# A hybrid decoder layer on one core: weights and mixed heads turned by VectorE and transfers instead of TensorE

## The chip, the cores and the metric

One core of a Trainium2 chip. The metric is the device time of one execution in microseconds (us). TensorE (PE) multiplies, with its weight loads (PEld) beside it; VectorE (DVE), ScalarE (ACT) and GpSimd (POOL) work on tiles; SyncE (SP) and POOL issue DMAs. Each engine takes its own list of instructions in order and waits on semaphores of the others.

## The reference

Cut to what is computed (x is 256 x 2048, one layer, 8 heads in each group):

```
h    = rmsnorm(x, ln1);  dq, dk, dv, sq, sk, sv = split(h @ w_in)          # 2048 x 6144
diff = softmax(q1 k1) v - lam * softmax(q2 k2) v      # causal, partial rotary on q and k
diff = rmsnorm(diff, per head) * (1 - lam_init)
a    = exp(log_sigmoid(z) + sum of log_sigmoid(-z) over later keys)        # strictly causal
sb   = rmsnorm(a @ sv, per head)
x    = x + concat(diff, sb) @ w_out                                        # 2048 x 2048
h    = rmsnorm(x, ln2);  x = x + relu(h @ w_mlp_in)**2 @ w_mlp_out         # 2048 x 8192 x 2048
out  = rmsnorm(x, ln_f)
```

## The kernel before

Every large product is fp32 split in two: an operand is hi + lo, and hi*hi, hi*lo and lo*hi are summed in PSUM (lines L260, L261, L262). The weights stream in as chunks of 512 rows by 512 columns (1 MB, tile w) into three buffers. Half a chunk is one job: ScalarE casts it into wh (L214), VectorE subtracts for wl (L217), and TensorE does 12 products of 128x512. Casts run three jobs ahead of the products, into four buffers each of wh and wl. Jobs 0 to 95 are the input projection, twelve blocks of eight jobs in the order dq0 dk0 dv0 dq1 dk1 dv1 sq0 sk0 sv0 sq1 sk1 sv1 (the digit is a group of four heads). From job 96 on comes the output projection: columns 0 and 1 (of four) with the rows of mixed heads 0 to 5 (jobs 96 to 107), then their last rows, which need mixT6 and mixT7 (jobs 108 to 111), then columns 2 and 3. The MLP follows.

Attention runs beside these jobs, as generators in a queue called side. After each job `tick` lets the first two of them run to their next yield; in jobs 96 to 107 it did so twice. What is called then only fixes the order in which instructions are handed over: a planner places them by a simulated time line, so an instruction that waits for its inputs there gets a later place in its engine's list.

- `prep_task` turns a q or k block: VectorE transposes blocks of 32x32 into the tile bl (L373, one buffer), 16 DMAs put them in place (L378, half from SP, half from POOL), and ScalarE copies the result into T (L396).
- `diff_task` does one head after another: scores (L443, L449), softmax of both maps and their difference w (L453 to L470), three TensorE transposes of w into PSUM (wtp, L475), a ScalarE copy to wT (L477), and the products with the values (L490).
- `sb_task` does two heads at once: scores (L503, L506), log of the break probabilities (L512 to L519), prefix sums by TensorE (L523 to L527), exponential (L531), values (L490).
- `finish_pair` normalises the output of two heads (L418 to L424), transposes it on TensorE (mtp, four transposes, L428), and splits it with the head gain into mixT (`split_pair`, L156 and L157).

Names carry a digit for group and head: s10 is the first head pair of the second stick-breaking group, s11 the second pair. mixT0 to mixT3 come from the softmax heads, mixT4 to mixT7 from the others; s10 makes mixT6 and s11 mixT7.

Of the kernel before, what the change touches and what calls it, by code (L numbers as in the profile page):

```python
# [10 lines left out]
F32 = mybir.dt.float32  # L11
# [7 lines left out]
P = 128  # L19
S = 256  # L20
D = 2048
DFF = 4 * D
NT = S // P
KT = D // P
NB = 512
CK = 4
HK = 2
HG = 4
# [16 lines left out]
def tile_hybrid_layer(  # L45
# [21 lines left out]
    nc = tc.nc  # L67
# [28 lines left out]
    ident = cpool.tile([P, P], F32, name="ident")  # L96
# [104 lines left out]
    def issue_conv():  # L201
        i = state["conv"]
        if i >= len(jobs):
            return
        c, h, _, _, pools = jobs[i]
        state["conv"] += 1
        if c is None:
            return
        w = wt[c][:, h * HK:(h + 1) * HK, :]
        pool = mlp["split"] if "split" in mlp and i % 3 == 2 else spool  # L210
        ph, pl = pools or ((pool, "wh"), (pool, "wl"))
        wh = ph[0].tile([P, HK, NB], F32R, tag=ph[1], name=f"wh{i}")
        for j in (range(HK) if i == 0 else (slice(0, HK),)):
            state["wh"] = nc.scalar.copy(wh[:, j], w[:, j])  # L214
        wl = pl[0].tile([P, HK, NB], F32R, tag=pl[1], name=f"wl{i}")
        for j in (range(HK) if i == 0 else (slice(0, HK),)):
            state["wl"] = nc.vector.tensor_tensor(wl[:, j], w[:, j], wh[:, j].bitcast(F32), op=ALU.subtract)  # L217
        sp[i] = (wh, wl)
        if h == CK // HK - 1:
            del wt[c]  # L220
            issue_dma()
# [4 lines left out]
    def tick(n=2):  # L226
        for task in list(side)[:n]:
            try:
                next(task)
            except StopIteration:  # L230
                side.remove(task)

    def run_jobs(upto, nside=2):
        while state["job"] < upto:
            i = state["job"]
            if i in hooks:
                hooks[i]()
            while state["conv"] < min(i + 1 + state["ahead"], len(jobs)):
                issue_conv()
            c, h, products, after, _ = jobs[i]  # L240
            products(h, *sp.pop(i, (None, None)))
            if after is not None:
                after()
            tick(nside)
            if n_proj <= i < n_out0:
                tick(nside)
            state["job"] += 1

# [26 lines left out]
    ps_tp = ctx.enter_context(tc.tile_pool(name="ps_tp", bufs=1, space=PSUM))  # L275
    attn = ExitStack()
    ap_ = attn.enter_context(tc.tile_pool(name="attn", bufs=2))
    ps_sc = attn.enter_context(tc.tile_pool(name="ps_sc", bufs=1, space=PSUM))
    ps_o = attn.enter_context(tc.tile_pool(name="ps_o", bufs=1, space=PSUM))
# [18 lines left out]
    ghd = cpool.tile([P, 1], F32, name="ghd")  # L298
    lamc = cpool.tile([P, 2], F32, name="lamc")
    epsc = cpool.tile([P, 1], F32, name="epsc")  # L300
    mostc = cpool.tile([P, 1], F32, name="mostc")
# [67 lines left out]
    def turn(dst, bl, src, engines):  # L369
# [6 lines left out]
        for i in range(4):  # L376
            for f in range(4):
                engines[(i * 4 + f) % len(engines)].dma_start(  # L378
                    dv[f * 32:(f + 1) * 32, :, i, :], bl[i * 32:(i + 1) * 32, :, f, :])


    grp = {}

# [30 lines left out]
    def finish_pair(o, g, kt2, name, **norm):  # L414

        ov = o.rearrange("p (g c) -> p g c", c=P)
        sq = ap_.tile([P, 4, P], F32, tag="sq", name=f"sq_{name}", bufs=1)
        nc.scalar.activation(sq, ov, AF.Square)  # L418
        ss = tiny.tile([P, 4], F32, tag="hss", name=f"hss_{name}")
        nc.vector.tensor_reduce(ss, sq, axis=AX.X, op=ALU.add)  # L420
        r = tiny.tile([P, 4], F32, tag="hr", name=f"hr_{name}")
        rsqrt_mean(ss, 4, P, name, r, **norm)
        on = ap_.tile([P, 4, P], F32, tag="on", name=f"on_{name}", bufs=1)
        nc.vector.tensor_tensor(on, ov, r.unsqueeze(2).broadcast_to([P, 4, P]), op=ALU.mult)  # L424
        yield
        tp = ps_tp.tile([P, 2 * S], F32, tag="tp", name=f"mtp_{name}")
        for i in range(4):
            nc.tensor.transpose(tp[:, i * P:(i + 1) * P], on[:, i, :], ident)  # L428
        yield
        mixT[kt2] = apool.tile([P, HK, 2, S], F32R, tag="act", name=f"mixT{kt2}")  # L430
        split_pair(mixT[kt2], tp, g, False)

    def diff_task(gi):
        while f"dk{gi}" not in grp:
            yield

        qT, kT, v = grp[f"dq{gi}"], grp[f"dk{gi}"], grp[f"dv{gi}", "src"]
        for h in range(HG):
            nm = f"d{gi}{h}"
            sc = ps_sc.tile([P, 2, 512], F32, tag="sc", name=f"sc_{nm}")  # L440

            for m in range(2):
                nc.tensor.matmul(sc[:, m, P:3 * P], identb, dmask, start=True, stop=False,  # L443
                                 skip_group_check=True)
            for cs, qs, ks, last in ((slice(0, S), slice(P, S), slice(0, S), False),
                                     (slice(S, S + P), slice(0, P), slice(0, P), True)):
                for m in range(2):
                    dm = slice(m * 64, (m + 1) * 64)
                    nc.tensor.matmul(sc[:, m, cs], qT[dm, h, qs], kT[dm, h, ks],  # L449
                                     start=False, stop=last, skip_group_check=True)  # L450
            yield
            nm4 = tiny.tile([P, 2, 2], F32, tag="nmax", name=f"nmax_{nm}")
            nc.vector.tensor_reduce(nm4[:, 1, :], sc[:, :, 0:S], axis=AX.X, op=ALU.max, negate=True)  # L453
            nc.vector.tensor_reduce(nm4[:, 0, :], sc[:, :, S:S + P], axis=AX.X, op=ALU.max, negate=True)
            e = ap_.tile([P, 2, 3 * P], F32, tag="e", name=f"e_{nm}", bufs=2)
            es = tiny.tile([P, 2, 2], F32, tag="es", name=f"es_{nm}")
            segs = {1: slice(0, S), 0: slice(S, S + P)}
            for qt in (1, 0):
                for m in range(2):
                    nc.scalar.activation(e[:, m, segs[qt]], sc[:, m, segs[qt]], AF.Exp,  # L460
                                         bias=nm4[:, qt, m:m + 1],
                                         accum_out=es[:, qt, m:m + 1])
            er = tiny.tile([P, 2, 2], F32, tag="er", name=f"er_{nm}")
            nc.vector.reciprocal(er, es)
            nc.vector.tensor_tensor(er, er, lamc.unsqueeze(1).broadcast_to([P, 2, 2]), op=ALU.mult)
            w = e[:, 0, :]
            for qt in (1, 0):
                s = segs[qt]
                nc.vector.tensor_scalar_mul(e[:, 1, s], e[:, 1, s], er[:, qt, 1:2])
                nc.vector.scalar_tensor_tensor(w[:, s], w[:, s], er[:, qt, 0:1], e[:, 1, s],  # L470
                                               op0=ALU.mult, op1=ALU.add)
            yield
            tp = ps_tp.tile([P, 2 * S], F32, tag="tp", name=f"wtp_{nm}")
            for i in range(3):
                nc.tensor.transpose(tp[:, i * P:(i + 1) * P], w[:, i * P:(i + 1) * P], ident)  # L475
            wT = ap_.tile([P, 3 * P], F32, tag="wT", name=f"wT_{nm}")
            nc.scalar.copy(wT, tp[:, :3 * P])  # L477
            yield
            if h % 2 == 0:
                o = ps_o.tile([P, 512], F32, tag="o", name=f"o_{nm}")  # L480
            pv_products(o, h, [wT[:, S:S + P]], [wT[:, 0:P], wT[:, P:S]], v)
            if h % 2 == 1:
                yield
                yield from finish_pair(o, ghd, (gi * HG + h) // 2, nm, eps=epsc, most=mostc)

    def pv_products(o, h, lhs0, lhs1, v):
        for qt, lhs in ((0, lhs0), (1, lhs1)):
            c0 = ((h % 2) * 2 + qt) * P
            for kb, l in enumerate(lhs):
                nc.tensor.matmul(o[:, c0:c0 + P], l, v[:, kb, h * P:(h + 1) * P],  # L490
                                 start=kb == 0, stop=kb == len(lhs) - 1)
# [86 lines left out]
    n_proj = len(jobs)  # L578
# [51 lines left out]
    n_out0 = len(jobs)  # L630
# [202 lines left out]
    with tc.manual_schedule(engines={mybir.EngineType.PE, mybir.EngineType.Activation, mybir.EngineType.DVE}):  # L833
        state["ahead"] = 0
        keep_clock_up(WARM0, "a")
        for step in START_ORDER.split():
            {"x": x_pair, "c": lambda i: issue_conv(), "m": lambda i: run_jobs(i + 1)}[step[0]](int(step[1]))
    state["ahead"] = AHEAD
    run_jobs(n_out0)
    while any(m is None for m in mixT):  # L840
        tick()
# [61 lines left out]
```

## Time and profile before

| | |
|---|---|
| median of three runs | 1110.95 us (1110.37 to 1111.13) |
| the profiled execution | 1109.93 us |
| its span, first to last instruction | 1108.2 us |
| TensorE busy | 1095.4 us, 99% |
| VectorE, ScalarE, POOL busy | 647.8, 519.4, 121.0 us |
| chain that ended last | PE 98% of the span |

The page gives for each engine the time in which it worked on something. A line of a timeline gives start and duration in us, engine, source line, operation, written tile <- read tiles, shape, count, and in brackets how long the engine had stood before it and who released it. Products are pipelined: one of 128x512 is shown with 0.39 us, while the next one starts 0.23 us after it; the distance of two starts is what one costs.

### The profile page before, as it was taken

How to read it: one execution, taken by the hardware profiler on the slowest of the kernel's cores; microseconds unless marked ns; L12 is line 12 of the kernel's file. 1: busy time of each engine (PE TensorE's matmuls, PEld its weight loads, DVE VectorE, ACT ScalarE, POOL GpSimd, SP SyncE). 2: the span in 40 equal slices, each digit the busy share in tenths (PEclk: the TensorE clock that was granted, in tenths of full speed). 3: DMA queues.
4: the chain of work that ended last, by engine and by line, in shares of the span. 5: the costliest groups of instructions: out<-in, count | busy, mean ns of one | idle time of the engine just before them, and what ended most of it. 6: DMA issues, size and time to landing. Idle time of an engine off the chain costs nothing.

```text
span 1108.2 us, 13750 instructions
## 1 busy us (share of the span) xinstructions
PE 1095.4 (99%) x5019; PEld 905.7 (82%) x5019; DVE 647.8 (58%) x798; ACT 519.4 (47%) x665; POOL 121.0 (11%) x240
## 2 busy tenths in 40 slices
PE   8999999999999999999999999999999999999996
PEld 6887888888887888888888888888888888888886
DVE  5756766656456665565554665545566544655752
ACT  5655555555555554444333444333444333444541
POOL 1111101101100212230001111000211000131000
PEclk9999999999999999999999999999999999999999
DMA  8675555646646885765666765656676566667512
GB/s 293 203 252 168 184 181 162 197 155 188 208 153 230 312 257 176 260 224 197 198 193 195 240 215 191 210 190 194 188 248 215 196 197 198 214 192 247 191 38 77
DMA packets 130296, 222.35 MB, mean 201 GB/s; under 512 B 11282, under 2 KB 26676, under 8 KB 130100
## 3 DMA queue, kind: packets, MB, share of 16 engines
q1 hardware_dynamic: 122772, 213.59, 58.3%
q0 software_dynamic: 7168, 7.35, 2.6%
q8 instruction: 39, 0.64, 0.2%
q10 hardware_dynamic: 288, 0.52, 0.1%
q14 instruction: 29, 0.24, 0.1%
HBM read 204.65 MB, written 2.10 MB: 187 GB/s over the span
## 4 chain that ended last, share of the span: by engine, by line
PE 98%; DMA 0%; DVE 0%; ACT 0%; SPq 0%; issue 0%; DVEq 0%; ACTq 0%
PE ia L260 10%; PE ia L262 10%; PE ia L261 10%; PE ma L261 10%; PE ma L262 10%; PE ma L260 10%; PE oacc L260 3%; PE oacc L262 3%; PE oacc L261 3%; PE acc_dk L260 1%; PE acc_dq L261 1%; PE acc_sk L260 1%; PE acc_sq L260 1%; PE acc_dq L262 1%; PE acc_sk L261 1%; PE acc_dq L260 1%
## 5 line engine op out<-in xcount | busy, mean ns | idle before, releaser
L217 DVE TENSOR_TENSOR wl<-w,wh 128x1024 fp32r<-128x1024 f32 (+1 forms) x385 | 468.7, 1221 | 393.7 <-ACT wh L214 392.7
L214 ACT CAST wh<-w 128x1024 fp32r<-128x1024 f32 (+1 forms) x385 | 402.2, 1049 | 501.8 <-PE ia L262 196.8
L261 PE MATMUL ia<-wl,xs 128*128 128x512 f32 x512 | 199.0, 389 | 0.0
L262 PE MATMUL ia<-wh,xs 128*128 128x512 f32 x512 | 198.6, 389 | 0.0
L260 PE MATMUL ia<-wh,xs 128*128 128x512 f32 x512 | 198.5, 389 | 0.0
L260 PE MATMUL ma<-wh,aT 128*128 128x512 f32 x480 | 186.3, 389 | 0.0
L261 PE MATMUL ma<-wl,aT 128*128 128x512 f32 x480 | 186.3, 389 | 0.0
L262 PE MATMUL ma<-wh,aT 128*128 128x512 f32 x480 | 185.5, 389 | 0.0
L378 POOL DMA_DIRECT2D hT<-bl x128 | 67.4, 535 | 529.9 <-DMA w<-in_w_mlp_in_dram 244.3
L262 PEld LDWEIGHTS ia<-wh,xs 128*128 128x128 f32 x512 | 96.1, 188 | 20.0
L261 PEld LDWEIGHTS ia<-wl,xs 128*128 128x128 f32 x512 | 96.1, 188 | 19.9
L260 PEld LDWEIGHTS ia<-wh,xs 128*128 128x128 f32 x512 | 96.1, 188 | 19.9
L260 PEld LDWEIGHTS ma<-wh,aT 128*128 128x128 f32 x480 | 90.1, 188 | 18.7
L261 PEld LDWEIGHTS ma<-wl,aT 128*128 128x128 f32 x480 | 90.1, 188 | 18.7
L262 PEld LDWEIGHTS ma<-wh,aT 128*128 128x128 f32 x480 | 90.1, 188 | 18.7
L260 PE MATMUL oacc<-wh,mixT 128*128 128x512 f32 x128 | 49.9, 391 | 1.3 <-ACT mixT L156 1.3
L261 PE MATMUL oacc<-wl,mixT 128*128 128x512 f32 x128 | 50.1, 392 | 0.0
L262 PE MATMUL oacc<-wh,mixT 128*128 128x512 f32 x128 | 49.4, 389 | 0.0
L378 POOL DMA_DIRECT2D x2T<-x2bl x32 | 16.8, 534 | 114.6 <-DVE x L615 72.7
L260 PEld LDWEIGHTS oacc<-wh,mixT 128*128 128x128 f32 x128 | 24.0, 188 | 6.3 <-ACT mixT L156 1.5
L261 PEld LDWEIGHTS oacc<-wl,mixT 128*128 128x128 f32 x128 | 24.1, 188 | 4.9
L262 PEld LDWEIGHTS oacc<-wh,mixT 128*128 128x128 f32 x128 | 24.0, 188 | 4.8
(227 smaller groups left out, 1219.9 us busy)
## 6 DMA issues: line engine op xcount, KB each, us to landing
w<-in_w_mlp_in_dram SPq DMA_DIRECT2D x64, 1024.0 KB, 5.4
w<-in_w_mlp_out_dram SPq DMA_DIRECT2D x64, 1024.0 KB, 5.1
w<-in_w_in_dram SPq DMA_DIRECT2D x46, 1024.0 KB, 5.1
w<-in_w_out_dram SPq DMA_DIRECT2D x16, 1024.0 KB, 5.4
hT<-bl SPq DMA_DIRECT2D x128, 32.0 KB, 1.9
hT<-bl POOLq DMA_DIRECT2D x128, 32.0 KB, 1.8
w<-in_w_in_dram SPq DMA_DIRECT2D x4, 512.0 KB, 7.7
x<-in_x_dram SPq DMA_DIRECT2D x3, 512.0 KB, 10.1
```

Of the source, the lines that this page charges most:

```text
L214: state["wh"] = nc.scalar.copy(wh[:, j], w[:, j])
L217: state["wl"] = nc.vector.tensor_tensor(wl[:, j], w[:, j], wh[:, j].bitcast(F32), op=ALU.subtract)
L260: nc.tensor.matmul(acc[t], a[:, 0, st], wh[:, j, :], start=s0, stop=False)
L261: nc.tensor.matmul(acc[t], a[:, 0, st], wl[:, j, :], start=False, stop=False)
L262: state["mm"] = nc.tensor.matmul(acc[t], a[:, 1, st], wh[:, j, :], start=False, stop=s1)
L378: engines[(i * 4 + f) % len(engines)].dma_start(dv[f * 32:(f + 1) * 32, :, i, :], bl[i * 32:(i + 1) * 32, :, f, :])
```

## The change

The three weight transposes on TensorE and the copy behind them are replaced by `turn_blocks`: one VectorE transpose of 32x32 blocks into the used second half of the tile e, and 16 DMAs (eight on SP, eight on POOL) straight into wT. The mixed heads are turned in the same way, through the tile bl and back into on, for all pairs but the last (mixT7), which keeps its TensorE transposes. Values products run one head behind the weights, since a turn now takes a round trip. In jobs 96 to 107 the queue is called four times a job instead of twice.

```diff
-            if n_proj <= i < n_out0:
+            for _ in range(3 if n_proj <= i < n_out0 else 0):
                 tick(nside)
...
+    def turn_blocks(dst, bl, src, n):
+        nc.vector.transpose(bl.rearrange("p f (k b) -> p f k b", b=32),
+                            src.rearrange("p (k f a) -> p f k a", k=n, f=4))
+        dv = dst.rearrange("p (k i b) -> p k i b", k=n, i=4)
+        for i in range(4):
+            for f in range(4):
+                (nc.gpsimd if f % 2 else nc.sync).dma_start(
+                    dv[f * 32:(f + 1) * 32, :, i, :],
+                    bl[i * 32:(i + 1) * 32, f, :].rearrange("a (k b) -> a k b", b=32))
...
-        yield
-        tp = ps_tp.tile([P, 2 * S], F32, tag="tp", name=f"mtp_{name}")
-        for i in range(4):
-            nc.tensor.transpose(tp[:, i * P:(i + 1) * P], on[:, i, :], ident)
+        if kt2 == KT // HK - 1:
+            yield
+            tp = ps_tp.tile([P, 2 * S], F32, tag="tp", name=f"mtp_{name}")
+            for i in range(4):
+                nc.tensor.transpose(tp[:, i * P:(i + 1) * P], on[:, i, :], ident)
+        else:
+            bl = ap_.tile([P, NT, 4, 4 * 32], F32, tag="bl", name=f"mbl_{name}", bufs=1)
+            tp = on.rearrange("p g c -> p (g c)")
+            turn_blocks(tp, bl[:, 0], tp, 4)
+            yield
+            yield
         yield
...
+        def values(h, nm, wT):
+            if h % 2 == 0:
+                o[0] = ps_o.tile([P, 512], F32, tag="o", name=f"o_{nm}")
+            pv_products(o[0], h, [wT[:, S:S + P]], [wT[:, 0:P], wT[:, P:S]], v)
+            if h % 2 == 1:
+                yield
+                yield from finish_pair(o[0], ghd, (gi * HG + h) // 2, nm, eps=epsc, most=mostc)
...
-            tp = ps_tp.tile([P, 2 * S], F32, tag="tp", name=f"wtp_{nm}")
-            for i in range(3):
-                nc.tensor.transpose(tp[:, i * P:(i + 1) * P], w[:, i * P:(i + 1) * P], ident)
+            bl = e[:, 1, :].rearrange("p (f c) -> p f c", f=4)
             wT = ap_.tile([P, 3 * P], F32, tag="wT", name=f"wT_{nm}")
-            nc.scalar.copy(wT, tp[:, :3 * P])
-            yield
-            if h % 2 == 0:
-                o = ps_o.tile([P, 512], F32, tag="o", name=f"o_{nm}")
-            pv_products(o, h, [wT[:, S:S + P]], [wT[:, 0:P], wT[:, P:S]], v)
-            if h % 2 == 1:
-                yield
-                yield from finish_pair(o, ghd, (gi * HG + h) // 2, nm, eps=epsc, most=mostc)
+            turn_blocks(wT, bl, w, 3)
+            yield
+            if last is not None:
+                yield from values(*last)
+            last = (h, nm, wT)
+        yield
+        yield
+        yield
+        yield from values(*last)
```

Where instructions stand now is shown at three places. The first is ScalarE's list around the copy T_sk1, the turned keys of the second stick-breaking group (the number behind wh is that of the half chunk, and so of the job that it serves). Before:

```order
L214 CAST wh94_2631<-w47_2525 128x1024
L214 CAST wh95_2647<-w47_2525 128x1024
L396 COPY T_sk1_2665<-src_sk1_2555 128x1024
L214 CAST wh96_2676<-w48_2562 128x1024
L214 CAST wh97_2701<-w48_2562 128x1024
L512 ACTIVATE t_s10_2692<-sc_s10_2667 128x768
```

The same list of the changed kernel around the same copy:

```order
L156 ACTIVATE mixT5_2729<-on_s01_2654,g2T_426 128x2x256
L214 CAST wh105_3131<-w52_2922 128x1024
L214 CAST wh106_3151<-w53_3025 128x1024
L214 CAST wh107_3167<-w53_3025 128x1024
L214 CAST wh108_3185<-w54_3101 128x1024
L407 COPY T_sk1_2839<-src_sk1_2726 128x1024
L214 CAST wh109_3201<-w55_3135 128x1024
```

The copy has moved from behind cast 95 to behind cast 108. The second place is TensorE's list at the prefix sums of s10 (negone and negtri_r are constants; oacc is the output projection). Before, they stand between products of job 98:

```order
L260 MATMUL oacc00_2750<-wh98_2719,mixT2_1736 128x512
L523 MATMUL sc_s10_2667<-t_s10_2692,negone_99 128x128
L261 MATMUL oacc00_2750<-wl98_2721,mixT2_1736 128x512
L262 MATMUL oacc00_2750<-wh98_2719,mixT2_1736 128x512
L260 MATMUL oacc01_2751<-wh98_2719,mixT2_1736 128x512
L261 MATMUL oacc01_2751<-wl98_2721,mixT2_1736 128x512
L262 MATMUL oacc01_2751<-wh98_2719,mixT2_1736 128x512
L525 MATMUL sc_s10_2667<-th_s10_2697,negtri_r_117 128x384
```

In the changed kernel the list reads there, from the last product of job 107 to the first of job 108:

```order
L262 MATMUL oacc11_3138<-wh107_3167,mixT5_2729 128x512
L552 MATMUL sc_s10_2841<-t_s10_2866,negone_99 128x128
L554 MATMUL sc_s10_2841<-th_s10_2871,negtri_r_117 128x384
L556 MATMUL sc_s10_2841<-tl_s10_2872,negtri_r_117 128x384
...
L519 MATMUL o_s10_2940<-src_sv1_2909,a_s10_2938 128x128 x6
...
L535 MATMUL sc_s11_3003<-T_sq1_2674,T_sk1_2839 128x128 x3
...
L556 MATMUL sc_s11_3003<-tl_s11_3018,negtri_r_117 128x384
L519 MATMUL o_s11_3047<-src_sv1_2909,a_s11_3045 128x128 x6
L260 MATMUL oacc00_2924<-wh108_3185,mixT6_3000 128x512
```

Before, the prefix sums and values of s10 and s11 lay spread among the products of jobs 98 to 107; now they stand in one piece between jobs 107 and 108, and the scores of s10 stand seven products ahead of that piece. The third place is TensorE's list ahead of job 105, in the changed kernel:

```order
L262 MATMUL oacc01_2925<-wh101_3021,mixT5_2729 128x512
L261 MATMUL oacc10_3137<-wl104_3117,mixT2_1975 128x512
L262 MATMUL oacc10_3137<-wh104_3115,mixT2_1975 128x512
L260 MATMUL oacc11_3138<-wh104_3115,mixT2_1975 128x512
L261 MATMUL oacc11_3138<-wl104_3117,mixT2_1975 128x512
L262 MATMUL oacc11_3138<-wh104_3115,mixT2_1975 128x512
L260 MATMUL oacc10_3137<-wh105_3131,mixT3_2270 128x512
```

Before, job 101 was done ahead of job 102; now its last product stands at the end of job 104, and wh105 takes the buffer of wh101.

## Rows read from the trace of the kernel before

**Rows 1.** The page: busy us of each engine, share of the span, instructions.

```profile
PE 1095.4 (99%) x5019; PEld 905.7 (82%) x5019; DVE 647.8 (58%) x798; ACT 519.4 (47%) x665; POOL 121.0 (11%) x240
```

**Rows 2.** Timeline of TensorE, around three weight transposes; start, duration, engine, line.

```profile
198.12 0.39 PE L260 MATMUL acc_sk<-wh,xs 128*128 128x512 f32 x1
198.35 0.49 PE L475 MATMUL wtp_d<-ident,e_d 128*128 128x128 f32 x3
...
199.15 0.39 PE L260 MATMUL acc_sk<-wh,xs 128*128 128x512 f32 x1
```

**Rows 3.** The same timeline, around the four transposes of a head pair.

```profile
122.08 0.40 PE L260 MATMUL acc_dk<-wh,xs 128*128 128x512 f32 x1
122.32 0.60 PE L428 MATMUL mtp_d<-ident,on_d 128*128 128x128 f32 x4
...
123.23 0.40 PE L260 MATMUL acc_dk<-wh,xs 128*128 128x512 f32 x1
```

**Rows 4.** Timeline of all engines, the steps of s10 from scores to exponential.

```profile
300.87 0.83 PE L506 MATMUL sc_s<-T_sq,T_sk 128*128 128x128 f32 x6
...
306.33 0.95 DVE L515 SCALAR_TENSOR_TENSOR t_s<-sc_s,t_s 128x768 f32<-128x768 f32 x1
...
307.97 0.84 ACT L518 CAST th_s<-t_s 128x768 fp32r<-128x768 f32 x1
...
309.24 0.95 DVE L519 TENSOR_TENSOR tl_s<-t_s,th_s 128x768 fp32r<-128x768 f32 x1
...
314.58 0.34 PE L527 MATMUL sc_s<-tl_s,negtri_r 128*128 128x384 f32 x1
...
315.54 0.81 ACT L531 ACTIVATE a_s<-sc_s 128x768 f32<-128x768 f32 x1 [2.63 <-PE sc_s L527]
```

**Rows 5.** The same, from the values of s10 to the norm of s11.

```profile
320.61 1.50 PE L490 MATMUL o_s<-src_sv,a_s 128*128 128x128 f32 x12
...
324.51 1.04 ACT L214 CAST wh<-w 128x1024 fp32r<-128x1024 f32 x1
...
325.58 1.23 DVE L217 TENSOR_TENSOR wl<-w,wh 128x1024 fp32r<-128x1024 f32 x1 [1.71 <-ACT wh L214]
...
327.34 0.96 DVE L515 SCALAR_TENSOR_TENSOR t_s<-sc_s,t_s 128x768 f32<-128x768 f32 x1
...
329.42 0.68 DVE L424 TENSOR_TENSOR on_s<-o_s,hr_s 128x512 f32<-128x512 f32 x1
...
340.79 1.50 PE L490 MATMUL o_s<-src_sv,a_s 128*128 128x128 f32 x12
...
344.68 0.30 ACT L138 ACTIVATE r_s<-lv_s,lnout_c 128x4 f32<-128x4 f32 x1
```

**Rows 6.** Timeline and tile view of a turn in the MLP.

```profile
439.31 1.31 DVE L373 STREAM_TRANSPOSE bl<-ia 128x512 f32<-128x512 f32 x2
440.64 5.07 SPq L378 DMA_DIRECT2D hT<-bl  x8
441.47 4.21 POOL L378 DMA_DIRECT2D hT<-bl  x8 [21.10 <-ACT wh L214]
...
DMA to landing us min/median/max: 1.7/1.9/6.3
```

**Rows 7.** Timeline of all engines, the wait for mixT7.

```profile
352.61 0.68 ACT L156 ACTIVATE mixT<-mtp_s,g2T 128x512 fp32r<-128x512 f32 x1
...
353.34 0.50 PE L260 MATMUL oacc<-wh,mixT 128*128 128x512 f32 x1 [1.28 <-ACT mixT L156]
```

**Rows 8.** Timeline of TensorE at the start, idle products of one form.

```profile
1.26 2.31 PE L296 MATMUL warm_a<-idle 128*128 128x512 bf16 x5 [1.26 <-DVE three_c L105]
...
4.98 1.03 PE L296 MATMUL warm_b<-idle 128*128 128x512 bf16 x4
```

**Rows 9.** Windows at the end: length, busy us of PE, PEld, DVE, ACT, POOL; granted clock.

```profile
1099.00:1100.00 1.00, 0.54 (x5) 0.34 (x3) 0.42 (x1) 0.00 (x0) 0.00 (x0) 1.00 0.00 0
1104.00:1105.00 1.00, 0.00 (x0) 0.00 (x0) 0.00 (x0) 0.00 (x0) 0.00 (x0) 0.50 1.01 363
```

More of the change, by code (lines that the diff above doesn't have):

```diff
@@ L437, in diff_task @@
         qT, kT, v = grp[f"dq{gi}"], grp[f"dk{gi}"], grp[f"dv{gi}", "src"]
+        o = {}
+        def values(h, nm, wT):
[5 more added lines that the diff above has]
+                yield from finish_pair(o[0], ghd, (gi * HG + h) // 2, nm, eps=epsc, most=mostc)
+        last = None
         for h in range(HG):
@@ L444, in diff_task @@
                                  skip_group_check=True)
-            for cs, qs, ks, last in ((slice(0, S), slice(P, S), slice(0, S), False),
-                                     (slice(S, S + P), slice(0, P), slice(0, P), True)):
+            for cs, qs, ks, end in ((slice(0, S), slice(P, S), slice(0, S), False),
+                                    (slice(S, S + P), slice(0, P), slice(0, P), True)):
                 for m in range(2):
@@ L449, in diff_task @@
                     nc.tensor.matmul(sc[:, m, cs], qT[dm, h, qs], kT[dm, h, ks],
-                                     start=False, stop=last, skip_group_check=True)
+                                     start=False, stop=end, skip_group_check=True)
             yield
```

## The prediction

> **What bounds the kernel now.** I read the page's busy shares first: TensorE is busy for 99% of the span, ScalarE for 47% and VectorE for 58% [rows 1]. TensorE carries one unbroken stream of products and sets the time: an edit is worth what it takes out of that stream or puts into it as a wait, and work on the other engines is free as long as nobody on TensorE waits for it. Then I read TensorE's timeline, for what a transpose takes from the stream, then the timeline of all engines around one stick-breaking head pair, for how long its chain of steps is when nothing else stands between them. Last I read the instruction order of both kernels, since each engine works its list off in order.
>
> **What leaves TensorE.** Starts in the stream lie 0.23 us apart, at a plain product as before the transposes. Around the three weight transposes of one head the starts at 198.12 and 199.15 enclose three products (two of them left out in the rows): 1.03 - 3 x 0.23 = 0.34 us for the transposes [rows 2]. Around the four mixed-head transposes 122.08 to 123.23 enclose three products too: 1.15 - 0.69 = 0.46 us [rows 3]. Eight heads and seven of the eight pairs lose theirs: 8 x 0.34 + 7 x 0.46 = 5.9 us less. The eight ScalarE copies out of PSUM go too; they lay beside products and return nothing.
>
> **What is added.** Fifteen turns: one VectorE transpose (0.66 us for 128x512, half of 1.31 [rows 6]) and 16 DMAs each, 240 in all, half on SP's queue, half on POOL's. VectorE has 42% idle, so 15 x 0.66 = 10 us there hide; without that cover they would cost those 10 us. A turn is over when its last DMA has landed: POOL issues eight in 4.21 us, the last about 0.53 us before 445.68, that is 4.5 us after the transpose ended at 440.62, and a landing takes 1.9 us, together 6.4 us [rows 6]. These are 512-byte runs, of which the change makes four times shorter ones, two (16 KB) per old one in number. Unknown cost: below, POOL's 0.53 us per issue stays or falls a little with the bytes; above, it doubles with the number of runs, and the turn takes 0.85 (POOL's start after the transpose) + 8 x 1.07 + 1.9 = 11.3 us. I take 6.4, from the only row of such a turn, and keep 11.3 for the range. On SP a turn's eight DMAs stand ahead of weight loads and hold them back by 5.1 us [rows 6]. A weight buffer comes free five half chunks (5 x 12 x 0.23 = 13.8 us) before its successor is split, and the split runs three more ahead of the product, so even two turns in a row on that queue (10 us) are hidden; I cost them at nothing. The values products of head 0 are the first that could wait: their turn stands behind the split of half chunk 30, which needs the buffer that job 26 gives back; from there 62 products (14.3 us) stand ahead of them, less cast, split and the turn's transpose (1.04 + 1.23 [rows 5] + 0.66): 11.4 us of room against 6.4 to 11.3, so no wait.
>
> **What the order does at the end.** The buffer bl exists once and is shared by the q and k turns and the new mixed-head turns, so these queue up behind one another, and the planner has laid them out in its order accordingly. In ScalarE's list the copy T_sk1 stood behind cast 95 and now stands behind cast 108. In TensorE's list the scores of s10 stood in front of the output projection; now they stand seven products before the end of job 107, and after those seven comes, with no product between, everything of s10 and s11: prefix sums, values, the next scores, prefix sums, values. Only then comes the first product with mixT6. The four rounds a job call the tasks early, but a call doesn't change what they must wait for, and the list has them late. So TensorE stands while ScalarE, VectorE and the queues walk through two head pairs. Counted from the start of the scores of s10:
>
> - To the start of VectorE's max-and-add on t: 306.33 - 300.87 = 5.5 us, with one cast between as now (wh111). Then 0.95, the cast th 0.84, the rest tl 0.95, prefix sums on TensorE until ScalarE starts on them 0.96, exponential 0.81: 10.0 us [rows 4].
> - From the values of s10 to the same place of s11: 327.34 - 320.61 = 6.7 us, less the cast of 1.04 that stood between and now doesn't: 5.7 [rows 4, 5]. Then t 0.95, on_s10 0.68 and its transpose 0.66 (both ahead of tl in VectorE's list, th beside them), tl 0.95, prefix sums 0.96, exponential 0.81: 10.7 us, so the values of s11 start at 20.7.
> - From these to the end of the exponential in the norm, which stands in ScalarE's list before mixT6: 344.98 - 340.79 = 4.2 us [rows 5], 24.9. The turn of s10 ended its transpose at 18.0 and has landed at 24.4, just hidden. Then mixT6's upper half, 0.68 us [rows 7]: TensorE goes on at 25.6.
>
> In these 25.6 us TensorE does scores 1.5, seven products 1.6, prefix sums twice 1.1, values with the next scores 3.1 and values 1.5, which it did before too: 9.9. It stands for 15.7 us more than before.
>
> **Two smaller terms.** Since mixT5 is late in the list, job 101 is mixed into job 104, and its last product stands six products before job 105, whose cast needs job 101's buffer (four of a kind). From there a cast of 1.04 and a split of 1.23 [rows 5] plus the end of the product (0.39) make 2.7 us, where products last six or seven times 0.23: 1.2 us of wait. In the place of the old 1.28 us wait for mixT7 [rows 7] the last pair now has its transpose two products ahead of need: ScalarE's 0.68 us, less 0.2 hidden by the products, 0.5; 0.8 less.
>
> **The clock.** Standing can cost twice. The granted clock was 0.50, the lower level of 1.2 GHz, at 1104 us, after TensorE's last product had ended by 1099.6 [rows 9]: it fell within 4.5 us of idling. It came up fast at the start: five idle products took 2.31 us from 1.26, four of the same form 1.03 us from 4.98 [rows 8], so it was back within 3.7 us. In the 25.6 us above TensorE idles up to 4 us at a stretch. Bounds: nothing, if the short steps hold the clock up; half of 3.7 us, 1.9, if it falls at the end and products come back at half rate; and 2.4 us on top if prefix sums and values of s11 run at half rate as well: 4.3. I take 1.9, the nearest row's. The Trainium skill (TensorE: Matmul & The Clock Gate, HAM oscillation) warns that TensorE left idle between bursts is throttled and each burst then starts cold; by it the 1.9 us belong in the sum, without it the sum would be 1.9 us smaller. The tail agrees that idling lowers the clock; no row here shows a gap with short steps in it.
>
> **Sum.** The profiled execution took 1109.9 us (span 1108.2 and 1.7 around it), 1.0 below the median of the runs. 1109.9 - 5.9 + 15.7 + 1.2 - 0.8 + 1.9 = 1122.0; on the median's footing 1123.0.
>
> **Rivals.**
> *The standing stretch is filled (faster).* If products behind the waiting ones could go first, or the chain took under 5 us, only the saving would be left: 1110.95 - 5.9 = about 1105. For it: 48 products of jobs 108 to 111 are due. Against: they need mixT6 or mixT7, which are what is waited for, and TensorE did stand for 1.28 us at mixT7 with later work in its list [rows 7]. It decides where the stretch falls below 4 us; no sum of the steps in rows 4 and 5 comes near.
> *The turns are slow everywhere (much slower).* If a turn took 20 us instead of 6.4 to 11.3, each of eight heads' values would come late, by 20 - 11.4 = 8.6 us where a head has as little room as head 0. With half of the heads at that: 4 x 8.6 = 34, and 20 - 6.4 = 13.6, of which 0.5 was hidden, at mixT6, on 1123: 1170. For it: the runs are 128 bytes, a quarter of those that rows 6 show. Against: each DMA carries half of the bytes of those in rows 6 or less, over the same two queues. A strided copy as a transpose is what the Trainium skill (VectorE: DVE Perf Modes, The three transpose paths) calls a trap, far slower than the crossbar's transpose; by that rule this case, with its 1170, would come true. No row shows a 128-byte run; with 512-byte runs the trace shows 1.9 us to landing.
> *The clock falls early (slower by more).* 4.3 instead of 1.9: 1125.4. It lies inside my range.
>
> **Chances and range.** Forecast, with the early fall of the clock as its upper part, 0.87; filled 0.06; a stretch no longer than what was saved 0.02; slow turns 0.05. Below: no clock term, no wait at job 105, a chain 3 us shorter by overlap: 1123 - 1.9 - 1.2 - 3 = 1117. Above: the turn of 11.3 us brings mixT6 4.4 us later, the early clock 2.4 more, and 1 for what I left out: 1131. Range 1116 to 1132. A measurement of this kernel can tell about 0.2% (2.2 us) from no change: faster 0.06, within it 0.02, slower 0.92.
>
> **What would show it.** TensorE's row should lose 52 transposes; its idle time should hold one cluster of about 16 us around 335 to 365 us, between the last product of job 107 and the first with mixT6, released by ScalarE and VectorE for s10 and s11, then by mixT6. Before it there should be one wait of about 1.2 us, at job 105. After it a stretch with a granted clock below 1.00 says that the clock term is right. I am wrong if the idle time there is under 6 us, if waits of DMA to wT at L519 add more than 2 us, or if the output projection ends earlier than it did.

## The result and the profile after

The changed kernel takes 1125.26 us (median; 1124.78 to 1128.25) against 1110.78 of the kernel before on the same chip: 1.0138 times as long over all runs (the two medians alone give 1.0130), 95% interval 1.0125 to 1.0150. Forecast were 1123.0 and 1116 to 1132. The profiled execution has a span of 1123.1 us, 14.9 more than before.

TensorE is still the bound. Its row of the page, to be read against [rows 1]:

```profile
PE 1098.5 (98%) x4967; PEld 906.7 (81%) x4967; DVE 654.0 (58%) x813; ACT 515.2 (46%) x657; POOL 185.9 (17%) x360
```

It has 52 instructions fewer and is busy 3.1 us longer; its idle time, span less busy, rose from 12.8 us [rows 1] to 24.6. Where the idle time lies is told by the timeline of TensorE from the scores of s10 to the first product with mixT7 (start, duration, engine, line; in brackets the idle time ahead of it and who ended it). It answers to [rows 4, 5, 7]:

```profile
328.91 0.83 PE L535 MATMUL sc_s<-T_sq,T_sk 128*128 128x128 f32 x6
...
331.76 0.39 PE L262 MATMUL oacc<-wh,mixT 128*128 128x512 f32 x1
335.41 0.49 PE L552 MATMUL sc_s<-t_s,negone 128*128 128x128 f32 x2 [3.26 <-DVE t_s L544]
336.27 0.44 PE L554 MATMUL sc_s<-th_s,negtri_r 128*128 128x384 f32 x1 [0.37 <-ACT th_s L547]
337.26 0.69 PE L556 MATMUL sc_s<-tl_s,negtri_r 128*128 128x384 f32 x1 [0.55 <-DVE tl_s L548]
...
339.92 2.93 PE L519 MATMUL o_s<-src_sv,a_s 128*128 128x128 f32 x12 [0.90 <-ACT a_s L560]
...
348.56 0.80 PE L552 MATMUL sc_s<-t_s,negone 128*128 128x128 f32 x2 [3.78 <-DVE t_s L544]
...
350.74 0.69 PE L556 MATMUL sc_s<-tl_s,negtri_r 128*128 128x384 f32 x1 [0.63 <-DVE tl_s L548]
...
353.39 2.93 PE L519 MATMUL o_s<-src_sv,a_s 128*128 128x128 f32 x12 [0.90 <-ACT a_s L560]
359.73 0.79 PE L260 MATMUL oacc<-wh,mixT 128*128 128x512 f32 x1 [3.41 <-ACT mixT L156]
...
360.74 0.63 PE L260 MATMUL oacc<-wh,mixT 128*128 128x512 f32 x1
361.17 0.63 PE L261 MATMUL oacc<-wl,mixT 128*128 128x512 f32 x1
...
368.23 0.50 PE L260 MATMUL oacc<-wh,mixT 128*128 128x512 f32 x1 [0.31 <-ACT mixT L156]
```

This is the cluster that was forecast, with the same releasers in the same order: eight gaps, the first of 3.26 us and the last of 3.41, 13.8 us together, between the last product of job 107 and the first with mixT6. The durations tell a second thing. The twelve values products took 1.50 us before [rows 5] and take 2.93 here, twice the time for the same work. The windows show why (length, busy us of PE, PEld, DVE, ACT, POOL, granted clock, DMA share and GB/s):

```profile
330.00:335.00 5.00, 2.15 (x12) 1.50 (x10) 2.02 (x3) 3.47 (x4) 0.00 (x0) 1.00 0.64 210
335.00:340.00 5.00, 2.77 (x9) 1.82 (x9) 1.31 (x2) 1.64 (x2) 0.00 (x0) 0.67 0.67 210
340.00:345.00 5.00, 4.78 (x26) 4.51 (x26) 1.03 (x3) 0.78 (x2) 0.00 (x0) 0.65 0.00 0
345.00:350.00 5.00, 1.38 (x3) 0.79 (x3) 3.08 (x8) 3.34 (x6) 0.00 (x0) 0.69 0.00 0
350.00:355.00 5.00, 3.47 (x13) 2.86 (x13) 0.68 (x1) 0.81 (x1) 4.34 (x8) 0.50 0.22 43
...
360.00:365.00 5.00, 5.00 (x14) 3.93 (x15) 1.44 (x2) 0.00 (x0) 0.00 (x0) 0.60 0.01 2
365.00:370.00 5.00, 4.69 (x23) 3.56 (x22) 2.83 (x3) 3.56 (x5) 0.00 (x0) 1.00 0.31 88
```

The granted clock was at 1.00 (2.4 GHz) up to 335 us and is at 1.00 again from 365 on. In between, the means over 5 us hide two falls. Read in steps of 1 us, the clock is at 0.50 (1.2 GHz) from 337 to 343 us, behind the first gap of 3.26 us; back at 1.00 from 344 to 346, at the end of the scores of s11 and in the idle time behind them; and at 0.50 once more from 347 to 363, having fallen inside the gap of 3.78 us. The products with mixT6 pay for it too: at 361 us their starts are 0.43 us apart, where products in the stream start 0.23 us apart.

That the scores of s10 begin so late has its reason further up. VectorE's transposes into the buffers of the turns (bl of q and k, mbl of mixed heads, one buffer here) in the changed kernel, from its timeline:

```profile
277.49 0.70 DVE L383 STREAM_TRANSPOSE mbl_s<-on_s 128x512 f32<-128x512 f32 x1
286.94 1.30 DVE L373 STREAM_TRANSPOSE bl_sq<-src_sq 128x512 f32<-128x512 f32 x2
300.86 0.70 DVE L383 STREAM_TRANSPOSE mbl_s<-on_s 128x512 f32<-128x512 f32 x1
311.16 1.30 DVE L373 STREAM_TRANSPOSE bl_sk<-src_sk 128x512 f32<-128x512 f32 x2
```

the last of these in the kernel before:

```profile
283.06 1.39 DVE L373 STREAM_TRANSPOSE bl_sk<-src_sk 128x512 f32<-128x512 f32 x2 [0.45 <-ACT src_sk L562]
```

and in the changed kernel the last instruction of ScalarE that writes its source:

```profile
274.70 0.69 ACT L591 ACTIVATE src_sk<-acc_sk,rstd 128x512 f32<-128x512 f32 x1
```

The turn of the keys sk1, which s10 cannot start without, now takes its place behind the turns of the mixed heads of s00 and s01, and starts 28 us later than before. In the kernel before it started when its source was there; here the source was there by 275.4 us, 36 us earlier.

### The profile page after: what moved, and what is told of

It reads as the page before. It is cut to its first block, busy times and chain, and to the rows that moved or that the text cites. A ratio compares the mean times of both kernels' runs of the same rounds, so it can differ in the third digit from the quotient of the medians.

```text
span 1123.1 us, 14184 instructions
## 1 busy us (share of the span) xinstructions
PE 1098.5 (98%) x4967; PEld 906.7 (81%) x4967; DVE 654.0 (58%) x813; ACT 515.2 (46%) x657; POOL 185.9 (17%) x360
## 4 chain that ended last, share of the span: by engine, by line
PE 97%; ACT 1%; DVE 1%; DMA 0%; issue 0%; DVEq 0%; SPq 0%; ACTq 0%
PE ia L262 10%; PE ia L260 10%; PE ia L261 10%; PE ma L261 10%; PE ma L260 10%; PE ma L262 10%; PE oacc L260 3%; PE oacc L261 3%; PE oacc L262 3%; PE acc_dq L262 1%; PE acc_dq L261 1%; PE acc_dk L260 1%; PE acc_dq L260 1%; PE acc_sk L261 1%; PE acc_sv L261 1%; PE acc_sk L260 1%
## 5 line engine op out<-in xcount | busy, mean ns | idle before, releaser
L388 POOL DMA_DIRECT2D wT_d<-e_d x64 | 34.4, 545 | 60.9 <-DVE e_d L383 28.3
L261 PEld LDWEIGHTS oacc<-wl,mixT 128*128 128x128 f32 x128 | 24.6, 192 | 5.1
```

The costliest lines, as they stand in the source:

```text
L261: nc.tensor.matmul(acc[t], a[:, 0, st], wl[:, j, :], start=False, stop=False)
L388: (nc.gpsimd if f % 2 else nc.sync).dma_start(dv[f * 32:(f + 1) * 32, :, i, :], bl[i * 32:(i + 1) * 32, f, :].rearrange("a (k b) -> a k b" ...
```

## The experiments

Two theories stood against each other. One: the shared buffer puts s10 and s11 into one place of TensorE's list, and TensorE pays for it with waits and with its clock. The other: the turns cost by themselves, by 240 DMAs of short runs on SP's and POOL's queues, or the four rounds do. All times are medians; ratios are against the kernel before on the same chip.

**A buffer of its own for the mixed heads' turn.**

```diff
-            bl = ap_.tile([P, NT, 4, 4 * 32], F32, tag="bl", name=f"mbl_{name}", bufs=1)
+            bl = ap_.tile([P, 4, 4 * 32], F32, tag="mbl", name=f"mbl_{name}", bufs=1)
...
-            turn_blocks(tp, bl[:, 0], tp, 4)
+            turn_blocks(tp, bl, tp, 4)
```

> The changed kernel, but the mixed heads' turn has a buffer of its own (128x512) instead of sharing the one of the q and k turns; then the whole of s10 and s11 stands spread between the products of the first jobs of the output projection again, and all 15 turns with their 240 DMAs stay. Theory (the shared buffer puts the two pairs behind the last product of job 107, and TensorE stands there): the stretch and its low clock go, the 5.9 us of the transposes stay saved, about 1105 us (1103 to 1107), and TensorE's longest idle time after the start is under 2 us. Rival (the turns themselves, by their DMAs, their queues or their landing, hold something up): at least 1120 us, little better than the 1125 of the changed kernel.

Measured: 1102.56 us, 0.9929 (0.9917 to 0.9942), faster than both kernels, and even below the theory's interval. The busy row of its page, and the longest row of TensorE's waits (engine, tile, line, who ended it: us, times, longest):

```profile
PE 1088.4 (99%) x4967; PEld 899.8 (82%) x4967; DVE 654.6 (59%) x813; ACT 513.7 (47%) x657; POOL 186.0 (17%) x360
```

```profile
PE oacc L260 <- ACT mixT L156: 1.3, 1, 1.3
```

and the turn of sk1 in VectorE's timeline, at 275.86 instead of 311.16:

```profile
275.86 1.39 DVE L373 STREAM_TRANSPOSE bl_sk<-src_sk 128x512 f32<-128x512 f32 x2 [0.16 <-ACT src_sk L591]
```

All 15 turns and their DMAs are there (POOL is as busy as in the changed kernel), and nothing waits for them. Of the waits behind the start only the old one for mixT7 is left. The rival, with at least 1120 us, falls.

**Only the softmax weights turned.**

```diff
-        if kt2 == KT // HK - 1:
+        if True:
```

> The changed kernel with the mixed heads' transposes on TensorE again, so that only the softmax weights are turned by VectorE and transfers (8 turns, 128 DMAs); nothing but the q and k turns then uses the shared buffer, and s10 and s11 stand between products as in the kernel before. Theory (shared buffer): the 8 x 0.34 = 2.7 us of the weight transposes are saved and nothing is lost, 1108 us (1107 to 1110). Rival (a turn costs by itself wherever it stands): 1111 us or more, since the 128 DMAs are there.

Measured: 1106.82 us, 0.9966 (0.9953 to 0.9978), just under the interval. Its row of the page:

```profile
PE 1092.6 (99%) x4995; PEld 902.9 (82%) x4995; DVE 650.6 (59%) x806; ACT 515.1 (47%) x657; POOL 155.4 (14%) x304
```

TensorE's busy time fell by 2.8 us [rows 1], where 2.7 were forecast for the 24 weight transposes. Against the own buffer's 1088.4 the 28 mixed-head transposes are worth 4.2, where 3.2 were forecast.

**Only the mixed heads turned, through the shared buffer.** The weights are transposed on TensorE as before, and the values products follow their own head again. The main lines against the changed kernel:

```diff
-            bl = e[:, 1, :].rearrange("p (f c) -> p f c", f=4)
+            tp = ps_tp.tile([P, 2 * S], F32, tag="tp", name=f"wtp_{nm}")
+            for i in range(3):
+                nc.tensor.transpose(tp[:, i * P:(i + 1) * P], w[:, i * P:(i + 1) * P], ident)
...
-            turn_blocks(wT, bl, w, 3)
+            nc.scalar.copy(wT, tp[:, :3 * P])
```

> The kernel before with the mixed heads' part of the change and the four rounds a job alone: weights are transposed on TensorE as before, 7 mixed-head turns go through the shared buffer. Theory (shared buffer): s10 and s11 again stand behind job 107 with nothing between; 7 x 0.46 = 3.2 us saved, about 21 us lost (12.8 of idle time and 8 of low clock as in the changed kernel), 1128 us (1125 to 1131). Rival (the weights' turns load the queues and cause the loss): no more than 1111 us.

Measured: 1132.38 us, 1.0194 (1.0180 to 1.0208). The direction is the theory's; the size is 1.4 us above its interval. The busy row of its page, and two windows of the stretch:

```profile
PE 1105.0 (98%) x4991; PEld 911.6 (81%) x4991; DVE 651.4 (58%) x805; ACT 519.8 (46%) x665; POOL 151.4 (13%) x296
```

```profile
345.00:350.00 5.00, 4.27 (x20) 4.15 (x21) 0.68 (x1) 1.27 (x2) 0.00 (x0) 0.50 0.00 0
...
365.00:370.00 5.00, 3.72 (x9) 2.95 (x10) 2.09 (x6) 0.92 (x2) 0.00 (x0) 0.50 0.01 2
```

The idle time is close to the changed kernel's (25.7 us against 24.6). The excess lies in the busy time: 1105.0 against 1095.4 - 4.2 = 1091.2 is 13.8 us, where the changed kernel has 10.1 over the one with its own buffer. The lower clock lasted longer here: summed over windows of 0.25 us it was granted for 27.3 us, against 23.9 in the changed kernel.

**Two rounds a job as before.**

```diff
-            for _ in range(3 if n_proj <= i < n_out0 else 0):
+            if n_proj <= i < n_out0:
```

> The changed kernel with two rounds a job in the early output projection, as before, instead of four. Theory (an early call does not change what a task must wait for): s10 and s11 stand in the same place of TensorE's list, 1125 us (1123 to 1127), with the same cluster of idle time of about 14 us. Rival (the four rounds are what brings the tasks together, or what keeps the loss down): a difference of over 3 us from the changed kernel to either side.

Measured: 1125.74 us, 1.0135 (1.0121 to 1.0148), the changed kernel's time. Its three largest waits of TensorE are the changed kernel's too, to the tenth:

```profile
PE sc_s L552 <- DVE t_s L544: 7.0, 2, 3.8
PE oacc L260 <- ACT mixT L156: 3.7, 2, 3.4
PE o_s L519 <- ACT a_s L560: 1.8, 2, 0.9
```

With the shared buffer in place the four rounds do nothing, neither good nor bad.

**Idle products inside the stretch.** The changed kernel with one function more, called behind the scores (n = 14), the prefix sums (3) and the last values (14):

```diff
+    def dummies(gi, mm, n, name):
+        if gi == 1:
+            warm = ps_tp.tile([P, 2 * S], F32, tag="tp", name=f"wm_{name}")
+            with tc.issue_after(mm.ins):
+                for _ in range(n):
+                    nc.tensor.matmul(warm, idle[:, :P], idle, start=True, stop=True)
```

> The changed kernel with 48 matmuls of zeros (bf16, 128x512) added to TensorE's list inside the standing stretch: 14 each behind the scores of s10 and of s11 and behind the values of s11, 3 behind each pair of prefix sums. They wait for nothing and nobody reads them; the rest of the list keeps its order, so the waits for VectorE and ScalarE stay. Theory (besides the idle time, about 10 us of the loss are work of TensorE at the lower clock, 10.1 being the busy time that the changed kernel has over the one with a buffer of its own): the granted clock stays at 1.00 from 330 to 365 us and the kernel takes 1115 us (1112 to 1119), though TensorE has more to do. Rival (the clock costs no more than the 1.9 us of the forecast; the rest is the chain's short steps): 1123 us or more, as the changed kernel or above it.

Measured: 1118.74 us, 1.0070 (1.0057 to 1.0084): TensorE has 48 matmuls more to do and the kernel is 6.5 us faster than without them. (The kernel before took 1110.66 beside the one and 1110.78 beside the other.) It lies inside the theory's interval, at its upper end. The stretch from the scores to the first product with mixT6:

```profile
329.32 0.83 PE L543 MATMUL sc_s<-T_sq,T_sk 128*128 128x128 f32 x6
...
338.44 1.60 PE L519 MATMUL o_s<-src_sv,a_s 128*128 128x128 f32 x12 [0.24 <-ACT a_s L570]
...
350.43 1.79 PE L519 MATMUL o_s<-src_sv,a_s 128*128 128x128 f32 x12
...
355.63 0.50 PE L260 MATMUL oacc<-wh,mixT 128*128 128x512 f32 x1 [0.39 <-ACT mixT L156]
...
362.12 0.50 PE L260 MATMUL oacc<-wh,mixT 128*128 128x512 f32 x1 [0.31 <-ACT mixT L156]
```

and windows of it, of which those left out have 1.00:

```profile
335.00:340.00 5.00, 4.21 (x28) 3.10 (x27) 2.18 (x2) 2.33 (x3) 0.00 (x0) 1.00 0.15 33
...
345.00:350.00 5.00, 3.36 (x10) 2.06 (x11) 2.48 (x4) 1.47 (x2) 2.75 (x6) 0.76 0.12 22
350.00:355.00 5.00, 5.00 (x28) 3.09 (x26) 1.38 (x6) 1.42 (x5) 1.59 (x3) 0.90 0.16 31
355.00:360.00 5.00, 4.61 (x21) 3.65 (x20) 1.74 (x4) 1.00 (x2) 0.00 (x0) 1.00 0.00 2
```

With the clock near 1.00 the chain takes 355.63 - 329.32 = 26.3 us, and 359.73 - 328.91 = 30.8 without the idle products. The products with mixT6, from there to the first with mixT7, take 6.5 us instead of 8.5. So 4.5 us of the loss were given back in the chain and 2.0 in the products behind it, 6.5 in all. It was not the whole of the clock, which did not stay at 1.00 as expected: it was at 0.50 from about 348 to 351 us, which the means of 0.76 and 0.90 hide.

**The place without the turning.** The kernel before, with no turn added; the second stick-breaking group held back.

```diff
-        while f"sk{gi}" not in grp:
+        while f"sk{gi}" not in grp or (gi == 1 and state["job"] < n_out0 - 1):
```

> The kernel before, every transpose on TensorE, no turn added; only the second stick-breaking group is held back until job 107, so that s10 and s11 stand behind its last product, s10 with nothing between its steps. Theory (the place in the list is what costs, not the turning): TensorE idles about 8.5 us up to the values of s10 and some 5 each at mixT6 and at mixT7, with work at the lower clock beside it, 1132 us (1126 to 1138). Rival (the loss needs the turns with their transfers): no more than 1115 us.

Measured: 1131.84 us, 1.0190 (1.0176 to 1.0204), at the theory's value. The waits:

```profile
PE mtp_s L428 <- DVE on_s L424: 4.9, 2, 4.0
PE sc_s L523 <- DVE t_s L515: 3.7, 1, 3.7
PE oacc L260 <- ACT mixT L156: 2.5, 2, 1.7
```

The sum agrees better than its parts. The gaps up to the values of s10 (3.73, 0.38, 0.30, 0.90) are 5.3 us, not 8.5, those around mixT6 and mixT7 2.7 and 4.7. The rest is busy time, 1107.1 us against 1095.4 [rows 1], under a clock granted at 0.50 to 0.53 from 345 to 355 us, for one. By the estimate that the next section explains, 8.8 of these 11.7 us are the clock. What stands: the place alone, with no turn, costs 21 us.

**Only the differential pairs and the weights turned, shared buffer kept.**

```diff
-        if kt2 == KT // HK - 1:
+        if kt2 >= KT // HK // 2:
```

> The changed kernel, but only the four pairs of the differential heads are turned by VectorE and transfers, through the shared buffer as in the change; the stick-breaking pairs go back to TensorE. 40 of the 52 transposes are gone. Theory (the buffer is harmful only where s10's turn stands in it behind the turns of the last q and k): s10 and s11 stand between products, nothing is lost, 40 x 0.15 = 6 us saved, 1104.5 us (1103 to 1107). Rival (any mixed-head turn in the shared buffer holds TensorE up): 1110 us or more.

Measured: 1102.72 us, 0.9926 (0.9913 to 0.9940), 0.3 us below the theory's interval, and the same as with a buffer of its own, within the 95% intervals. Its row of the page, and the turn of sk1 in VectorE's timeline:

```profile
PE 1090.3 (99%) x4979; PEld 901.9 (82%) x4979; DVE 651.7 (59%) x810; ACT 514.3 (47%) x657; POOL 172.8 (16%) x336
```

```profile
271.06 1.39 DVE L373 STREAM_TRANSPOSE bl_sk<-src_sk 128x512 f32<-128x512 f32 x2 [0.45 <-ACT src_sk L591]
```

Twelve transposes more than with the own buffer cost 1.9 us of busy time, and no wait for mixT7 is left. That s10 stands earlier may be the reason; no run shows it. Sharing the buffer is no harm as such; it was harmful where the mixed heads of s00 and s01 stood in it ahead of the turn that s10 needs.

## Why the prediction was right, and which terms were off

**The mechanism** was right: 52 transposes left, the two pairs stood in one piece behind job 107, and TensorE waited there for VectorE and ScalarE in the order given. The own buffer removes that place and the whole loss; before_late makes it by itself. Taking the changed kernel and the one with its own buffer as the two ends, the span's 14.9 us come apart as follows:

| term | forecast | measured | from |
|---|---|---|---|
| transposes | -5.9 | -7.0 | busy 1095.4 to 1088.4, own buffer |
| standing at mixT6 | +15.7 | +13.8 | eight gaps |
| wait at job 105 | +1.2 | 0 | no such wait |
| wait for mixT7 | -0.8 | -1.0 | 1.28 [rows 7] to 0.31 |
| clock (measured: all added busy time) | +1.9 | +10.1 | busy 1088.4 to 1098.5 |
| idle at the start | 0 | -1.1 | a wait for x, not in the change |
| sum | +12.1 | +14.8 | span +14.9 |

The total came out better than its parts: the clock was short by 8.2 us, and the other rows together were 5.5 too high. That the size came so close is in part luck; the direction, the place and the order of the waits are not.

**The clock is the mis-sized term.** The forecast took 1.9 us, half rate for the first products after the stretch. This part was right: the products with mixT6 gave back 2.0 us with the idle products. (Its source, [rows 8], shows the low clock at the start by durations alone; the profile's granted clock reads 1.00 there, from 0 to 7 us.) What it put at nothing, and at 2.4 us only in the rival "the clock falls early", is TensorE's own work inside the stretch. There the clock fell behind the first gap already: s10's prefix sums from 337 us on and its values, and s11's prefix sums and values, ran at half rate. The idle products show 6.5 us of the clock's cost directly. An estimate from the granted clock, in windows of 0.25 us from 320 to 380 us: TensorE's busy time, times 1 less the granted clock, adds up to 7.9 us in the changed kernel and to 1.7 with the idle products. The difference, 6.2, is close to the 6.5 measured. So of the 10.1 us some 8 are the clock, and some 2 are other busy time; the ends of products that nothing follows closely, which count as busy, are among it. The estimate is rough: in the run with two rounds it comes to 10.0, with only 1.3 us more busy time than in the changed kernel. The rival had the right sign, but its 4.3 us are half of it; that its 1125.4 us meets the 1125.26 is chance, since other terms were too high. The Trainium skill (TensorE: Matmul & The Clock Gate, HAM oscillation) warned that bursts with idle time between them run throttled, and the trace agrees: 2.93 us for twelve products that take 1.50 at the full clock.

**The chain.** Forecast 25.6 us from the scores of s10 to the first product with mixT6; 30.8 in the changed kernel, 26.3 where the clock was held up but for some 3 us. The step sum from [rows 4, 5] was good to 0.7 us there. What it lacked is that TensorE's steps in the chain slow down with the clock that falls in it: its work was put at 9.9 us and took 17.0, the 30.8 less 13.8 of gaps. Slow work counts as busy, which is in part why the idle time was below its forecast.

**The wait at job 105** did not come: TensorE's waits list none for ScalarE's cast or VectorE's split there. Its premise, that wh105 takes the buffer of wh101, is not what ran. In ScalarE's list the casts 105 to 108 stand between mixT5 and T_sk1; by that order the first line is cast 105 and the third is casts 107 and 108. The second line is the last product of job 101, the fourth the first of job 105:

```profile
314.37 1.05 ACT L214 CAST wh<-w 128x1024 fp32r<-128x1024 f32 x1 [1.04 <-PE oacc L262]
...
320.98 0.39 PE L262 MATMUL oacc<-wh,mixT 128*128 128x512 f32 x1
...
321.40 2.19 ACT L214 CAST wh<-w 128x1024 fp32r<-128x1024 f32 x2 [3.25 <-PE oacc L262]
...
322.33 0.39 PE L260 MATMUL oacc<-wh,mixT 128*128 128x512 f32 x1
```

Cast 105 was done 7 us before job 105. The cast that started when job 101 ended is that of job 107, whose products begin at 327.77 us.

**The transposes** were worth 7.0, not 5.9. The weights' term was right (2.8 against 2.7); the mixed heads' 0.46 was read at one pair [rows 3], and over seven it is 4.2 / 7 = 0.60.

**The turns** cost what was taken, nothing. Landing and issue of the turn of mixed heads, from the tile view (DMA to landing; POOL's instructions, ns min/median/max):

```profile
L388 POOL DMA_DIRECT2D on_s<-mbl_s x24: 548/548/558, 278.8 to 354.2; - x24
...
DMA to landing us min/median/max: 1.7/3.5/4.6
```

The issue did not double with the number of runs: 0.55 us, where [rows 6] had 0.53. The landing was 3.5 us in the median, where the forecast took the 1.9 of a turn in the MLP. The shorter runs don't explain the difference: the same turns landed in 1.8 us with the buffer of their own, and in the kernel before the turns of sk, with runs of 512 bytes, took 4.5 (medians of the tile views of on_s and src_sk). It had no effect on TensorE: before mixT6 ScalarE's norm ended last, and no wait for a landing is listed there. The rival of slow turns (1170) is refuted by the own buffer's 1102.56. The Trainium skill (VectorE: DVE Perf Modes, The three transpose paths), which was named for it, speaks of a plain DMA copy that does the transposing by its strides, with a large innermost stride at the destination. Here VectorE transposes the blocks and the DMAs write contiguous runs of 128 bytes, so the warning does not bear on this change, and no run here tests it.

**The filled stretch** failed on what was said against it: 24 products of jobs 108 to 111 need mixT6, the other 24 mixT7.

## What to carry to other kernels

A buffer that exists once puts its users in a queue; before giving it another user, ask which later turn stands behind the new one and who on the bounding engine needs that turn. A saving of 7 us on the bound became a loss of 14.5 because one turn slid back by 28 us, and a second buffer of 2 KB a partition gave it back. When a chain of short steps is laid bare on TensorE, price its gaps, its own work at the lower clock too, and the first products behind it: here 13.8, some 6 and 2 us.

## What was not expected of the hardware

The granted clock moved up and down inside the stretch. The twelve values products of s10 ran at half rate (2.93 us from 339.92), but the scores of s11 right behind them got faster while they ran, 1.15 us for the six of the first head and 0.83, as in [rows 4], for those of the second:

```profile
342.85 1.15 PE L535 MATMUL sc_s<-T_sq,T_sk 128*128 128x128 f32 x6
...
343.94 0.83 PE L535 MATMUL sc_s<-T_sq,T_sk 128*128 128x128 f32 x6
```

Behind the next gap, of 3.78 us, the prefix sums of s11 were slow again. So this chain paid for the clock twice. And 48 matmuls of zeros, which compute nothing, made the kernel 6.5 us faster, nearly as much as the transposes that the change took away.
